# Delta rule: two chunks of a pair share their small operations, and a pair's inverses are fetched ahead of the doubling that reads them

## The chip, the cores and the metric

One NeuronCore of a Trainium2 chip runs one program. The metric is device time in microseconds (us), the median of a few executions; smaller is better. The engines are PE (TensorE, matrix products), DVE (VectorE), ACT (ScalarE), POOL (GpSimd) and SP (SyncE, which here only issues DMAs). Each runs its own instructions in a fixed order and waits on semaphores.

## The reference, cut to what matters

Two decoder layers over 2048 prompt tokens and 8 single sample tokens, everything in float32. The change concerns the gated delta rule of the first layer (4 heads of 128 channels; q, k, v, a decay g and a step beta per token). Per chunk of tokens:

```python
gc = jnp.cumsum(g, axis=-1)
decay = jnp.where(incl, jnp.exp(jnp.where(incl, diff, 0.0)), 0.0)
a_low = jnp.where(strict, jnp.einsum('bhnid,bhnjd->bhnij', kb, k) * decay, 0.0)
sol = lax.linalg.triangular_solve(a_low + jnp.eye(c), rhs, left_side=True, lower=True, unit_diagonal=True)
...
def step(s, xs):                       # over the chunks, one after the other
    v_new = u_n - w_n @ s
    o_n = qd_n @ s + qk_n @ v_new
    s = s * gl_n + kd_n.T @ v_new
```

q and k are l2-normalized before, and o is rms-normalized per token and head and multiplied by silu(z) after. The output then goes with a convolution branch through an output projection, followed by memory attention, a second layer and a last norm.

## The kernel before, in words

Large products run as three float32r products (high and low halves of both sides), so most of the time is PE time. The stages in order of time: products of the memory keys and values (to about 100 us), the input projection with its convolutions (to about 820 us), the delta rule (about 776 to 1208 us), the output projection `e2`, attention, the second layer.

Nothing is ordered by hand. A class `Flow` (line 56) keeps an estimated clock for every engine while the program is built. "Dense" code emits large products; side tasks are Python generators, and `pump` (line 342) steps a side task as soon as the estimate says that its inputs are there and its condition holds. So a changed size, condition or count moves instructions on all engines, and each engine then runs its list in that order whatever the real times are. `move` and `rows` (lines 191 and 201) put a copy on ACT or DVE by the estimated load, `ve` (line 210) on DVE or POOL. A DMA of a tile that only ACT wrote is issued by ACT, the others by SP.

The delta rule is `phase2` (line 1057), with 16 chunks of 128 tokens in 8 pairs. Beside it the dense work is `Fill` (line 990), 576 products that fold attention weights, the tiles `rhi` and `rlo` in the trace. The side tasks of the delta rule:

- `prep(n)` (line 1103), three at a time, one chunk each: loads k, q, v, forms the decay (`dec`), the matrix A = k k^T scaled by beta and the decay, and the products that the scan needs. The squared norms are in `ss`, and `br` holds four-column factors made by short DVE chains: a Newton inverse square root `rsqrt` (line 410, 11 DVE operations on [128, 4]) and five others. Chunks 0 to 3 may start when the pool `cq` is open; from chunk 4 on they need `dx`, which opens once the input projection has freed its last buffers.
- `inv16(t)` (line 1192): POOL inverts the 16x16 diagonal blocks of pair t.
- `levels(t)` (line 1215): sends these inverses into the tile `UT` by eight small DMAs, one per head and chunk, then doubles block size 16 to 32, 64, 128 on PE. One pair after the other.
- `scan()` (line 1295): the recurrence over the chunks, with the state in four tiles `S`.
- `onorms(i)` (line 1342), two tasks, one for even and one for odd chunks: the output norm, with 13 DVE operations on [128, 4], a multiplication by z, and a store to `d_b`.

`places` (line 1386) opens pools; `e2` can use its large tiles when all inverses are done, chunk 13 is scanned and the fill has ended.

Of the kernel before, what the change touches and what calls it, by code (L numbers as in the profile page):

```python
# [436 lines left out]
def spread(F, C, pool, ppool, r, n, tag, dg=None):  # L437
# [7 lines left out]
    ps = ppool.tile([128, 512], F32, tag="bg", name="ps_bc")  # L445
# [206 lines left out]
def phase1(F, C, I, D, st, P, R, mmp, bgp, loaders, mix, hp):  # L652
# [269 lines left out]
    def conv4(b, t):  # L922
# [11 lines left out]
        F.dma(D.qkv[b][:, t * 512:(t + 1) * 512], z)  # L934
# [122 lines left out]
def phase2(F, C, I, D, st, P, fill, hp, mmp, bgp, after):  # L1057
# [30 lines left out]
    slots, vfree = Res(SL), Res(3)  # L1088
# [1 line left out]
    done = {"A": set(), "T": set(), "L": set(), "S": {-1}, "N": set(), "P": set(), "U": set()}  # L1090
# [203 lines left out]

    def scan():
# [5 lines left out]
        for n in range(16):  # L1301
# [40 lines left out]
    def onorms(i):  # L1342
        for n in range(i, 16, 2):
            yield lambda: n in oq
            o, ss = oq.pop(n)
# [1297 lines left out]
```

## Time and profile before

| | us |
|---|---|
| median of 3 runs (2899.82 to 2907.46) | 2905.99 |
| the profiled execution | 2902.86 |
| its span, first to last instruction | 2901.1 |

Of the span PE is busy 2730.5 us, DVE 1968.4, ACT 1032.0 and POOL 657.0. Busy PE time is counted at the clock that PE was granted, so a slow stretch reads as busy. The profiled execution is 3.1 us under the median.

### The profile page before, as it was taken

To read this page: it belongs to the slowest core of one execution; us is meant where nothing else is said; L and a number is where in the kernel's file an instruction comes from. 1 tells how busy PE (TensorE), PEld (TensorE's weight loads), DVE (VectorE), ACT (ScalarE), POOL (GpSimd) and SP (SyncE) were. 2 spreads that over 40 slices of the span, in tenths; PEclk is the share of its full clock that TensorE was granted. 3 is DMA by queue.
4 is the path that set the end of the run, shared out by engine and by line. 5 is a ranking of instruction groups with operands and counts; after the bars stand their busy time and mean duration, and the time that the engine had idled before them with its cause. 6 is when DMAs were issued, how large, how long until landed. Compare 5 with 4: busy or idle time off the path is not lost.

```text
span 2901.1 us, 52440 instructions
## 1 busy us (share of the span) xinstructions
PE 2730.5 (94%) x20202; PEld 2498.5 (86%) x20202; DVE 1968.4 (68%) x4612; ACT 1032.0 (36%) x2448; POOL 657.0 (23%) x936
## 2 busy tenths in 40 slices
PE   7999999999998889799999999899999998999997
PEld 6878888888888778699898889899999997789987
DVE  6838999988667887776655556867755445765453
ACT  5632232233356455432321325443422122432321
POOL 3301112111054355122232320111011111221210
PEclk9999999999989899899999999999999999999998
DMA  7611122123455557565645434322545556422211
GB/s 240 213 48 41 46 75 65 46 77 113 129 148 160 154 165 230 172 228 183 211 149 169 144 117 140 116 70 74 173 134 165 181 165 206 136 78 68 70 59 52
DMA packets 269194, 377.85 MB, mean 130 GB/s; under 512 B 46096, under 2 KB 168208, under 8 KB 268944
## 3 DMA queue, kind: packets, MB, share of 16 engines
q1 hardware_dynamic: 211776, 264.77, 29.4%
q0 software_dynamic: 20864, 67.39, 7.5%
q10 hardware_dynamic: 36304, 42.34, 4.2%
q8 instruction: 159, 2.61, 0.4%
q14 instruction: 91, 0.75, 0.1%
HBM read 276.38 MB, written 96.40 MB: 128 GB/s over the span
## 4 chain that ended last, share of the span: by engine, by line
PE 34%; DMA 9%; DVE 6%; issue 2%; ACT 1%; POOL 1%; DVEq 0%; SPq 0%; POOLq 0%; ACTq 0%
PE ps_mm L168 32%; DMA a_big<-d_sp 2%; DVE a_big L225 1%; DMA a_big<-d_sq 1%; DMA a_big<-in_cache_v 1%; PE ps_pt L172 1%; DMA w_f<-d_x 1%; DVE rlo L225 1%; DVE w_d L219 1%; DMA rraw<-d_VW 1%; PE ps_row L168 1%; DVE rlo L219 1%; DVE ml L219 0%; DMA rraw<-d_G 0%; DMA a_big<-in_cache_k 0%
## 5 line engine op out<-in xcount | busy, mean ns | idle before, releaser
L219 POOL TENSOR_TENSOR rlo<-rraw,rhi 128x512 fp32r<-128x512 f32 x143 | 209.1, 1470 | 579.0 <-ACT rhi L186 495.5
L225 DVE SCALAR_TENSOR_TENSOR cacc<-glu,dww,cacc 128x1024 f32<-128x1024 f32 x240 | 325.6, 1369 | 5.9 <-ACT cacc L186 1.4
L219 POOL TENSOR_TENSOR w_sqb<-w_sqb,w_sqq 128x512 f32<-128x512 f32 (+1 forms) x101 | 137.1, 1357 | 660.9 <-ACT w_sqq L186 653.9
L168 PE MATMUL ps_mm<-xh,rhi 128*128 128x256 f32 (+1 forms) x1920 | 274.0, 285 | 5.3 <-DVE pool_sm L219 3.2
L168 PE MATMUL ps_mm<-xl,rhi 128*128 128x256 f32 (+1 forms) x1920 | 273.1, 284 | 0.0
L168 PE MATMUL ps_mm<-xh,rlo 128*128 128x256 f32 (+1 forms) x1920 | 272.7, 283 | 0.0
L168 PEld LDWEIGHTS ps_mm<-xh,rhi 128*128 128x128 f32 x1920 | 250.6, 192 | 8.6 <-issue 3.4
L168 PEld LDWEIGHTS ps_mm<-xl,rhi 128*128 128x128 f32 x1920 | 250.0, 192 | 2.6
L168 PEld LDWEIGHTS ps_mm<-xh,rlo 128*128 128x128 f32 x1920 | 248.2, 191 | 1.0
L168 PE MATMUL ps_mm<-hh,rhi 128*128 128x512 f32 (+2 forms) x1152 | 216.8, 329 | 20.2 <-ACT hh L186 15.8
L219 DVE TENSOR_TENSOR w_y<-ps_mm,w_y 128x256 f32<-128x256 f32 (+1 forms) x248 | 103.4, 420 | 165.6 <-PE ps_mm L168 161.2
L168 PE MATMUL ps_mm<-hh,rlo 128*128 128x512 f32 (+2 forms) x1152 | 214.6, 328 | 0.0
L168 PEld LDWEIGHTS ps_mm<-hh,rhi 128*128 128x128 f32 x1152 | 177.9, 191 | 42.0 <-ACT hh L186 16.2
L168 PE MATMUL ps_mm<-hl,rhi 128*128 128x512 f32 (+2 forms) x1152 | 211.7, 326 | 0.0
L225 DVE SCALAR_TENSOR_TENSOR a_big<-a_big 128x256 f32<-128x256 f32 x256 | 105.0, 448 | 144.5 <-DMA a_big<-d_sp 78.3
L186 ACT ACTIVATE rhi<-rraw 128x512 fp32r<-128x512 f32 x235 | 143.8, 628 | 164.0 <-DMA rraw<-d_G 41.5
L168 PEld LDWEIGHTS ps_mm<-hh,rlo 128*128 128x128 f32 x1152 | 175.9, 191 | 19.4 <-issue 2.2
L168 PEld LDWEIGHTS ps_mm<-hl,rhi 128*128 128x128 f32 x1152 | 175.4, 190 | 17.3
L168 PE MATMUL ps_mm<-mh,rhi 128*128 128x256 f32 (+1 forms) x1152 | 170.1, 288 | 11.8 <-ACT mh L186 11.7
L168 PE MATMUL ps_mm<-ml,rhi 128*128 128x256 f32 (+1 forms) x1152 | 170.5, 290 | 2.5 <-DVE ml L219 2.5
L168 PEld LDWEIGHTS ps_mm<-mh,rhi 128*128 128x128 f32 x1152 | 153.6, 195 | 14.5 <-ACT mh L186 12.8
L168 PE MATMUL ps_mm<-mh,rlo 128*128 128x256 f32 (+1 forms) x1152 | 165.6, 284 | 0.0
(425 smaller groups left out, 5344.5 us busy)
## 6 DMA issues: line engine op xcount, KB each, us to landing
w_f<-d_x SPq DMA_DIRECT2D x60, 512.0 KB
d_x<-w_y SPq DMA_DIRECT2D x44, 512.0 KB
w_y<-d_x SPq DMA_DIRECT2D x44, 512.0 KB
a_big<-in_cache_k POOLq DMA_DIRECT2D x64, 256.0 KB, 4.0
a_big<-in_cache_v POOLq DMA_DIRECT2D x64, 256.0 KB, 4.1
rraw<-in_w_in SPq DMA_DIRECT2D x56, 256.0 KB
d_qkv<-so ACTq DMA_DIRECT2D x48, 256.0 KB
rraw<-in_w_xk SPq DMA_DIRECT2D x32, 256.0 KB
```

The source lines that it names most:

```text
L168: self.nc.tensor.matmul(out, lhsT, rhs, start=start, stop=stop)
L172: self.nc.tensor.transpose(out, in_, ident)
L186: self.nc.scalar.activation(out=out, in_=in_, func=func, scale=scale, **kw)
L219: self._e(eng).tensor_tensor(out=out, in0=a, in1=b, op=op)
L225: self._e(eng).scalar_tensor_tensor(out=out, in0=a, scalar=s, in1=b, op0=op0, op1=op1, **kw)
```

## The change

1. The eight squared norms of a pair stand in one tile `ss`, interleaved by head and chunk, and all chains in `br` run once a pair on [128, 8], in the prep of the odd chunk. The even chunk waits for it (`done["K"]`, `done["B"]`, `done["R"]`). `onorms(t)` handles a pair too.
2. A new task `spread16(t)` does the eight DMAs into `UT` (now two buffers) ahead of `levels(t)`, which waits for an entry in `uts`.
3. The buffers of the late pool `dx` serve chunks 6 and 7 of each eight in place of 4 and 5, so chunks 4 and 5 may start before `dx` opens.
4. q, k, v, z and b lie in DRAM so that a chunk's four heads are one 2 KB run a partition (q, k, v, z) when read. The writers (`fin_z`, `conv4`) now write runs of 512 bytes in place of 2 KB, and `fin_z` issues more DMAs.
5. `spread` takes its PSUM pool from the work object at the time of use.

```diff
@@ fin_z, conv4 @@
-            F.dma(D.z[b][:, o:o + n], z[:, 0:n])
+            a = o
+            while a < min(o + n, SEQ):
...
+                    F.dma(D.z[c:c + k, :, b, :].rearrange("c p t -> p c t"), z[:, a - o:a - o + 128 * k].rearrange("p (c t) -> p c t", c=k))
...
-        F.dma(D.qkv[b][:, t * 512:(t + 1) * 512], z)
+        F.dma(D.qkv[b // 4, 4 * t:4 * t + 4, :, b % 4, :].rearrange("c p t -> p c t"), z.rearrange("p (c t) -> p c t", c=4))
@@ room, prep @@
-        q, b = (dx, 2) if n % 8 in (4, 5) else (cq, SL - 2)
+        q, b = (dx, 2) if n % 8 in (6, 7) else (cq, SL - 2)
...
-        yield lambda: nxt[0] == n and cq and (n < 4 or dx) and slots.n >= 2 - n % 2 and (n < SL or n // 2 - (SL+1)//2 in done["T"])
+        yield lambda: nxt[0] == n and cq and (n < 6 or dx) and slots.n >= 2 - n % 2 and (n < SL or n // 2 - (SL+1)//2 in done["T"])
...
-        F.dma(X.k, qkv[1][:, :, tok])
+        F.dma(X.k, D.qkv[1, n])
...
-        yield
+        done["K"].add(n)
+        yield lambda: n - c2 in done["K"]
...
-        br = X.br = cq.tile([128, 12], F32, tag="br", name="br", bufs=SL)
-        F.ts(br[:, 0:4], ss[:, 4:8], EPS, ALU.add)
-        F.recip(br[:, 4:8], br[:, 0:4])
-        F.tt(br[:, 4:8], br[:, 4:8], st.beta[:, :, n], ALU.mult)
-        F.stt(br[:, 8:12], br[:, 4:8], -1.0, gate["egc"][:, :, n], ALU.mult, ALU.mult)
+        if c2:
+            br = X.br = hu[n - 1].br = cq.tile([128, 32], F32, tag="br", name="br", bufs=SL // 2)
+            F.ts(br[:, 0:8], ss[:, 8:16], EPS, ALU.add)
+            F.recip(br[:, 8:16], br[:, 0:8])
...
+            done["B"].add(n // 2)
...
-        yield
+        yield lambda: n // 2 in done["B"]
...
-        rsqrt(F, cq, br[:, 4:8], br[:, 0:4], 4, "pr")
-        F.tt(br[:, 4:8], br[:, 4:8], st.beta[:, :, n], ALU.mult)
-        yield
+        if c2:
+            rsqrt(F, cq, br[:, 24:32], br[:, 0:8], 8, "pr")
...
+            done["R"].add(n // 2)
+        yield lambda: n // 2 in done["R"]
@@ levels @@
+    uts = {}
+
+    def spread16(t):
+
+        yield lambda: lp and t in done["T"] and (t < 2 or 2 * t - 4 in done["L"])
         ux = hu[2 * t].ux
-        UT = lp.tile([128, 8, 48], F32, tag="UT", name="UT", bufs=NL)
+        UT = lp.tile([128, 8, 48], F32, tag="UT", name="UT", bufs=2)
         F.memset(UT[:, :, 32:48], 0.0)
         for g in range(8):
             F.dma(UT[:, g, 0:32], ux[8 * g:8 * g + 8].rearrange("p r t k -> p r (t k)"))
+        uts[t] = UT, F.cur
+        F.now()
         done["U"].add(t)
+
+    def levels(t):
+        yield lambda: t in uts
+        U = A = hu[2 * t].A2.rearrange("p c h j -> p (c h) j")
+        UT, F.cur = uts.pop(t)
@@ onorms @@
-    def onorms(i):
-        for n in range(i, 16, 2):
-            yield lambda: n in oq
...
-            rsqrt(F, sq, f, os, 4, f"o{i}")
+    def onorms(t):
+        yield lambda: {2 * t, 2 * t + 1} <= set(oq)
...
+        rsqrt(F, sq, f, os, 8, "o")
@@ build @@
-        D.qkv = dr.tile([12, 128, SEQ], F32, name="d_qkv")
-        D.z = dr.tile([4, 128, NT], F32, name="d_z")
+        D.qkv = dr.tile([3, 16, 128, 4, 128], F32, name="d_qkv")
+        D.z = dr.tile([16, 128, 4, 128], F32, name="d_z")
+        D.zs = dr.tile([128, 4, 8], F32, name="d_zs")
...
-        D.b = [dr.tile([4, 128, gn(g)], F32, name=f"d_b{g}") for g in range(NG)]
+        D.b = [dr.tile([128, 4, gn(g)], F32, name=f"d_b{g}") for g in range(NG)]
```

What the planner makes of it, at three places. On DVE, the chain of `rsqrt` in one prep of the first chunks; `br` are the factors, `rt` and `ri` its scratch. Before:

```order
L415 TENSOR_SCALAR ri<-br 128x4
L234 TENSOR_SCALAR br<-ri 128x4
L219 TENSOR_TENSOR rt<-br 128x4
L225 SCALAR_TENSOR_TENSOR rt<-rt,br 128x4
L225 SCALAR_TENSOR_TENSOR br<-rt,br 128x4
L219 TENSOR_TENSOR rt<-br 128x4
L225 SCALAR_TENSOR_TENSOR rt<-rt,br 128x4
L225 SCALAR_TENSOR_TENSOR br<-rt,br 128x4
L219 TENSOR_TENSOR rt<-br 128x4
L225 SCALAR_TENSOR_TENSOR rt<-rt,br 128x4
L225 SCALAR_TENSOR_TENSOR br<-rt,br 128x4
L219 TENSOR_TENSOR br<-br,beta 128x4
```

and with the change:

```order
L415 TENSOR_SCALAR ri<-br 128x8
L234 TENSOR_SCALAR br<-ri 128x8
L219 TENSOR_TENSOR rt<-br 128x8
L225 SCALAR_TENSOR_TENSOR rt<-rt,br 128x8
L225 SCALAR_TENSOR_TENSOR br<-rt,br 128x8
L219 TENSOR_TENSOR rt<-br 128x8
L225 SCALAR_TENSOR_TENSOR rt<-rt,br 128x8
L225 SCALAR_TENSOR_TENSOR br<-rt,br 128x8
L219 TENSOR_TENSOR rt<-br 128x8
L225 SCALAR_TENSOR_TENSOR rt<-rt,br 128x8
L225 SCALAR_TENSOR_TENSOR br<-rt,br 128x8
L219 TENSOR_TENSOR br<-br,beta 128x8
```

The chain keeps its 12 operations, on eight columns in place of four, and stands once for two chunks. Over the program DVE has 4193 instructions in place of 4358: 232 fewer of these small ones, and 67 more of other kinds, mostly copies that the planner takes from ACT. PE has the same 18457.

On PE, where the second preps begin; `ident,gc` and `ident,k` are the first matmuls of a chunk, `hh` and `hl` the last group of the input projection, `rhi`/`rlo` the fill. Before, chunks 4, 5 and 6 begin together after the fill has started:

```order
L168 MATMUL ps_mm<-rhi,rlo 128x512 x2
L168 MATMUL ps_bg<-b_7977 32x32 x16
L168 MATMUL ps_bg<-ident,gc 128x128 x4
L172 MATMUL ps_bg<-ident,k 128x128 x4
L168 MATMUL ps_bg<-ident,gc 128x128 x4
L172 MATMUL ps_bg<-ident,k 128x128 x4
L168 MATMUL ps_bg<-ident,gc 128x128 x4
L172 MATMUL ps_bg<-ident,k 128x128 x4
```

With the change chunks 4 and 5 begin inside the last group of the input projection:

```order
L168 MATMUL ps_mm<-hl_236,rhi 128x260 x8
L168 MATMUL ps_mm<-hh_235,rlo 128x260 x8
L168 MATMUL ps_bg<-ident,gc 128x128 x4
L172 MATMUL ps_bg<-ident,k 128x128 x4
L168 MATMUL ps_mm<-hh_235,rhi 128x260 x4
L168 MATMUL ps_bg<-ident,gc 128x128 x4
L172 MATMUL ps_bg<-ident,k 128x128 x4
L172 MATMUL ps_bg<-ident,q 128x128 x4
```

The first matmul of chunk 4 has 54 fill products ahead of it before, and none with the change; 146 of the large products that stood ahead of it now stand behind.

On PE, the end of the delta stage; `S` is the state, `vn` the new values, `xh` and `xl` the first products of `e2`. Before, the last chunk's scan stands directly ahead of `e2`, and the last fill product 35 rows above `xh`:

```order
L168 MATMUL ps_bg<-S_7426,q_12977 128x128
L168 MATMUL ps_bg<-S_7427,q_12977 128x128
L168 MATMUL ps_bg<-S_7428,q_12977 128x128
L168 MATMUL ps_bg<-x,A 128x128 x4
L168 MATMUL ps_mean<-w_sqa,ones 128x256
L168 MATMUL ps_bg<-vn,kd 128x128 x4
L168 MATMUL ps_bg<-vn,qk 128x128 x4
L172 MATMUL ps_bg<-ident,o 128x128 x4
L168 MATMUL ps_ss<-ones,w_sqa 128x64 x2
L168 MATMUL ps_mm<-xh,rhi 128x264 x8
```

With the change the fill reaches to `e2`:

```order
L168 MATMUL ps_mm<-rhi,rlo 128x512 x2
L168 MATMUL ps_mm<-rhi 128x512 x2
L168 MATMUL ps_mm<-rlo,rhi 128x512 x2
L168 MATMUL ps_mm<-rhi,rlo 128x512 x2
L168 MATMUL ps_bc<-w_sqq,ones 128x256
L168 MATMUL ps_mm<-rhi 128x512 x2
L168 MATMUL ps_mm<-rlo,rhi 128x512 x2
L168 MATMUL ps_mm<-rhi,rlo 128x512 x2
L172 MATMUL ps_bg<-ident,o 128x128 x4
L168 MATMUL ps_mm<-xh,rhi 128x264 x8
L168 MATMUL ps_mm<-xl,rhi 128x264 x8
```

The last scan product (`vn,qk`) now has 36 fill products behind it, before none; the last product of the last pair's inverse has 168 behind it, before none.

## Rows read from the trace of the kernel before

**Rows 1.** The page, part 1 (busy us, share of the span, instructions) and the line of part 2 that gives the granted TensorE clock in tenths in 40 slices of 72.5 us.

```profile
PE 2730.5 (94%) x20202; PEld 2498.5 (86%) x20202; DVE 1968.4 (68%) x4612; ACT 1032.0 (36%) x2448; POOL 657.0 (23%) x936
...
PEclk9999999999989899899999999999999999999998
```

**Rows 2.** Busy time of each engine by stretch (from:to, length, then busy us and instructions of PE, PEld, DVE, ACT, POOL; then the granted clock, the DMA engines' mean busy share, GB/s).

```profile
820.00:1164.00 344.00, 299.52 (x3726) 268.96 (x3724) 264.14 (x811) 192.22 (x653) 169.37 (x324) 0.91 0.61 174
1164.00:1200.40 36.40, 23.35 (x175) 21.12 (x175) 29.62 (x74) 19.42 (x50) 5.55 (x6) 0.76 0.59 177
1200.40:1240.00 39.60, 34.06 (x247) 33.13 (x247) 28.32 (x72) 15.98 (x31) 2.84 (x3) 0.92 0.50 164
1240.00:1440.00 200.00, 194.58 (x1493) 184.45 (x1491) 137.72 (x311) 67.22 (x113) 55.36 (x64) 1.00 0.66 215
```

**Rows 3.** Who ended the idle time of PE between 820 and 1200.4 us: us in total, times, longest.

```profile
PE ps_bg L168 <- DVE S L225: 11.3, 5, 4.3
PE ps_bg L168 <- DVE lo L232: 9.7, 4, 4.3
PE ps_bg L168 <- DVE A L232: 8.9, 4, 3.3
PE ps_bg L168 <- ACT vn L186: 5.7, 3, 3.1
...
PE ps_bg L168 <- DVE x L225: 3.0, 2, 2.6
```

**Rows 4.** PE in order of time at the end of the delta stage: start, us, what, and in brackets the idle time before it.

```profile
1164.04 0.69 PE L168 MATMUL ps_bg<-b 32*32 32x32 f32 x32
1168.07 0.65 PE L168 MATMUL ps_bg<-A 64*64 64x64 f32 x8 [3.33 <-DVE A L232]
...
1187.63 1.26 PE L168 MATMUL ps_bg<-x,A 128*128 128x128 f32 x8 [2.61 <-DVE x L225]
...
1199.54 1.12 PE L168 MATMUL ps_ss<-ones,w_sqa 128*128 128x64 f32 x4 [4.96 <-POOL w_sqa L219]
1200.41 2.11 PE L168 MATMUL ps_mm<-xh,rhi 128*128 128x264 f32 x8
```

**Rows 5.** DVE groups by form between 820 and 1240 us: the small operations on four numbers a partition (count, busy us, mean ns, idle before).

```profile
L225 DVE SCALAR_TENSOR_TENSOR of<-rt,of 128x4 f32<-128x4 f32 x48 | 12.0, 249 | 1.7
...
L225 DVE SCALAR_TENSOR_TENSOR rt<-rt,os 128x4 f32<-128x4 f32 x48 | 10.2, 212 | 1.6
...
L225 DVE SCALAR_TENSOR_TENSOR br<-rt,br 128x4 f32<-128x4 f32 x36 | 8.7, 242 | 1.2
L225 DVE SCALAR_TENSOR_TENSOR rt<-rt,br 128x4 f32<-128x4 f32 x36 | 8.5, 237 | 1.2
L234 DVE TENSOR_SCALAR ss<-ss 128x4 f32<-128x4 f32 x16 | 8.4, 526 | 0.0
...
L219 DVE TENSOR_TENSOR br<-br,beta 128x4 f32<-128x4 f32 x24 | 8.2, 341 | 0.8
```

**Rows 6.** DVE in order of time within one such chain, then one row of POOL from the same microseconds.

```profile
972.06 0.16 DVE L225 SCALAR_TENSOR_TENSOR rt<-rt,br 128x4 f32<-128x4 f32 x1
972.26 0.16 DVE L225 SCALAR_TENSOR_TENSOR br<-rt,br 128x4 f32<-128x4 f32 x1
...
973.43 2.73 DVE L225 SCALAR_TENSOR_TENSOR br<-rt,br 128x4 f32<-128x4 f32 x1
976.19 0.17 DVE L219 TENSOR_TENSOR br<-br,beta 128x4 f32<-128x4 f32 x1
...
973.66 2.48 POOL L219 TENSOR_TENSOR rlo<-rraw,rhi 128x512 fp32r<-128x512 f32 x2
```

**Rows 7.** DVE, the whole trace, by form: the same operation on eight numbers a partition, from the sample group.

```profile
L225 DVE SCALAR_TENSOR_TENSOR a_r<-rt,a_r 128x8 f32<-128x8 f32 x9 | 1.5, 167 | 0.3
```

**Rows 8.** DVE groups by form between 820 and 1240 us: operations that a planner can put on DVE or ACT (POOL for the second).

```profile
L238 DVE CAST rhi<-rraw 128x512 fp32r<-128x512 f32 x38 | 18.3, 493 | 1.8 <-DMA rraw<-in_w_xqT 1.8
...
L219 DVE TENSOR_TENSOR rlo<-rraw,rhi 128x512 fp32r<-128x512 f32 x24 | 16.8, 715 | 2.7 <-ACT rhi L186 2.7
...
L232 DVE TENSOR_SCALAR gv<-ps_mm,g_x 128x256 f32<-128x256 f32 x23 | 10.6, 480 | 9.3 <-DMA d_G<-gv 7.0 <-ACT gv L186 2.0 <-DMA d_VW<-gv 0.3
...
L238 DVE COPY ad<-A 32x128 f32<-32x128 f32 x22 | 5.5, 252 | 0.3
...
L238 DVE COPY b<-ps_bg 32x256 f32<-32x256 f32 x10 | 4.0, 411 | 2.3 <-PE ps_bg L168 2.0 <-ACT b L186 0.2
```

**Rows 9.** The tile UT, whole trace: its DMA issues on SP (ns min/median/max of one issue, first and last).

```profile
L313 SPq DMA_DIRECT2D UT<-x x64: 604/605/867, 817.9 to 1139.6; - x64
```

**Rows 10.** DMA queues (packets, MB, share of 16 engines): SP's between 820 and 1200.4 us, then ACT's between 200 and 700 us; then a wait of ACT between 200 and 820 us.

```profile
q1 hardware_dynamic: 89594, 56.82, 52.4%
...
q10 hardware_dynamic: 8928, 14.75, 8.1%
...
ACT so L186 <- DMA d_qkv<-so: 4.2, 2, 2.2
```

**Rows 11.** ACT between 820 and 1240 us: the group that rounds weights, with what ended its idle time.

```profile
L186 ACT ACTIVATE rhi<-rraw 128x512 fp32r<-128x512 f32 x58 | 35.8, 630 | 31.6 <-DMA rraw<-in_w_out_e 9.2 <-DMA rraw<-in_w_xqT 7.0 <-DMA rraw<-d_G 5.3
```

**Rows 12.** PE: the first matmuls of chunk 6 and of chunk 7, partners of one pair, in order of time.

```profile
844.25 1.33 PE L168 MATMUL ps_bg<-ident,gc 128*128 128x128 f32 x8 [2.51 <-DVE A L232]
...
896.10 1.06 PE L168 MATMUL ps_bg<-ident,gc 128*128 128x128 f32 x8
```

More of the change, by code (lines that the diff above doesn't have):

```diff
@@ L444, in spread @@
     yield
-    ps = ppool.tile([128, 512], F32, tag="bg", name="ps_bc")
+    ps = getattr(ppool, "bgp", ppool).tile([128, 512], F32, tag="bg", name="ps_bc")
     F.mm(ps[:, 0:n], C.ones, dg[:, 0:n])
@@ L772, in fin_z @@
             F.act(z[:, 0:n], ps[:, 0:n], AF.Silu)
-            F.dma(D.z[b][:, o:o + n], z[:, 0:n])
+            a = o
+            while a < min(o + n, SEQ):
+                c, r = divmod(a, 128)
+                e = min(o + n, SEQ)
+                if r == 0 and e - a >= 128:
+                    k = (e - a) // 128
+                    F.dma(D.z[c:c + k, :, b, :].rearrange("c p t -> p c t"), z[:, a - o:a - o + 128 * k].rearrange("p (c t) -> p c t", c=k))
+                    a += 128 * k
+                else:
+                    k = min(128 - r, e - a)
+                    F.dma(D.z[c, :, b, r:r + k], z[:, a - o:a - o + k])
+                    a += k
+            if o + n > SEQ:
+                F.dma(D.zs[:, b, :], z[:, SEQ - o:NT - o])
         fin = {"z": fin_z}
@@ L1087, in phase2 @@
     SL = 8
[L1088 removed]
+    slots, vfree, afree = Res(SL), Res(3), Res(3)
     nxt = [0]
[L1090 removed]
+    done = {"A": set(), "T": set(), "L": set(), "S": {-1}, "N": set(), "P": set(), "U": set(), "B": set(), "R": set(), "K": set()}
     inext = [0]
@@ L1108, in prep @@
         X.ia = cq.tile([64, 16, 16], F32, tag="a16", name="a16", bufs=(SL + 1) // 2) if n % 2 == 0 else hu[n - 1].ia
+        ss = X.ss = cq.tile([128, 16], F32, tag="ss", name="ss", bufs=8) if n % 2 == 0 else hu[n - 1].ss
         X.A2 = room("A", n) if n % 2 == 0 else hu[n - 1].A2
         X.A = X.A2[:, n % 2]
-        tok = slice(128 * n, 128 * n + 128)
         X.k = room("k", n)
@@ L1123, in prep @@
         F.tt(dec, C.negm.unsqueeze(1).to_broadcast([128, 4, 128]), pd, ALU.subtract)
-        ss = X.ss = cq.tile([128, 8], F32, tag="ss", name="ss", bufs=16)
+        c2 = n % 2
         pk = ps4()
@@ L1151, in prep @@
         for h in range(4):
-            F.stt(X.A[:, h, :], pa[:, h, :], br[:, 4 + h:5 + h], dec[:, h, :], ALU.mult, ALU.mult)
-        yield vfree.ok
+            F.stt(X.A[:, h, :], pa[:, h, :], br[:, 8 + 2 * h + c2:9 + 2 * h + c2], dec[:, h, :], ALU.mult, ALU.mult)
+        yield lambda: vfree.ok() and afree.ok()
         vfree.take()
+        afree.take()
         v = small("v", 2 * NP, 3)
-        F.dma(v, qkv[2][:, :, tok])
+        F.dma(v, D.qkv[2, n])
         F.now()
@@ L1174, in prep @@
             F.dma(X.ia[i:i + 8], a16[:, h, :])
+        afree.give()
         done["A"].add(n)
@@ L1187, in prep @@
         X.bv = room("bv", n)
-        F.rows(X.bv, pv, br[:, 4:8])
+        F.rows(X.bv, pv, hk(br[:, 24:32])[:, :, c2])
         vfree.give()
@@ L1340, in scan @@
             F.dma(D.o_delta_p[h], S[h])
[L1342 to L1347 removed]
+    def onorms(t):
+        yield lambda: {2 * t, 2 * t + 1} <= set(oq)
+        os = sq.tile([128, 8], F32, tag="os", name="os", bufs=1)
+        o, z = [], []
+        for c in range(2):
+            oc, ss = oq.pop(2 * t + c)
+            o.append(oc)
+            z.append(sq.tile([128, 4, 128], F32, tag=f"z{c}", name="z", bufs=1))
+            F.dma(z[c], D.z[2 * t + c])
             F.now()
[L1349 removed]
+        for c in range(2):
             for h in range(4):
                 j = sq.tile([128, 128], F32, tag="junkq", name="junkq", bufs=1)
[L1352 removed]
+                F.act(j, o[c][:, h, :], AF.Square, accum=os[:, 2 * h + c:2 * h + c + 1])
             yield
[L1355 to L1360 removed]
+        F.ts(ss[:, 0:8], ss[:, 0:8], EPS, ALU.add, EPS * 128, ALU.mult)
+        F.stt(os, os, 1.0 / 128, ss[:, 0:8], ALU.mult, ALU.add)
+        f = sq.tile([128, 8], F32, tag="of", name="of", bufs=1)
+        rsqrt(F, sq, f, os, 8, "o")
+        yield
+        for c in range(2):
+            n = 2 * t + c
+            F.rows(o[c], o[c], f.rearrange("p (h c) -> p h c", c=2)[:, :, c])
             yield
@@ L1378, in phase2 @@
         F.spawn(every(levels, i, NL, 8), 2)
+    F.spawn(every(spread16, 0, 1, 8), 2)
     for i in range(NI):
         F.spawn(every(inv16, i, NI, 8), 2)
-    for i in range(2):
-        F.spawn(onorms(i), 1)
+    F.spawn(every(onorms, 0, 1, 8), 1)
     for i in range(NP):
@@ L1486, in tok_spread @@
 def tok_spread(F, C, W, r, n):
-    return spread(F, C, W.p, W.bgp, r, n, "w", dg=W.t("sqq", [128, ceil128(n)]))
+    return spread(F, C, W.p, W, r, n, "w", dg=W.t("sqq", [128, ceil128(n)]))
 def mm3(F, R, W, name, j, x, n):
```

41 lines of the change are left out of this document (16 added, 25 removed).

## The prediction, made before the changed kernel had run

> **What bounds the kernel now.** I read the page first: PE is busy 94% of the span, and its granted clock falls to eight tenths only in slices 12, 14 and 17 of 40, which lie between 798 and 1233 us, and in the last slice [rows 1]. That stretch is the delta stage. The table of stretches gives its losses. Busy time multiplied by the granted clock is about what the same work takes at full clock; what is left of a stretch's length is loss. 820 to 1164 us: 344.0 - 299.5 x 0.91 = 71.4 us lost. 1164 to 1200.4 us: 36.4 - 23.35 x 0.76 = 18.7. 1200.4 to 1240 us: 39.6 - 34.06 x 0.92 = 8.3. The 200 us after that lose 5.4 [rows 2]. So 98 us in the delta stage and its exit could be won, and PE's instructions are the same before and after: the change can only win idle time and slow clock.
>
> Whom does PE wait for? Mostly DVE: for S 11.3 us, lo 9.7, A 8.9, x 3.0, and for ACT's vn 5.7 [rows 3]. DVE is busy 264 of the 344 us, 77% [rows 2]. DMAs hardly appear among PE's waits. After 1164 us the fill is used up and PE has only the last pair's inverse and the last two scans, each step waiting for DVE, until the first product of e2 at 1200.41 [rows 4]. Its clock stood at 1.2 in place of 2.4 GHz for about half of that stretch, the mean granted clock being 0.76 [rows 2].
>
> **Part 1, the shared chains.** Per chunk 16 small DVE operations in prep and 13 in the output norm go: 29 x 16 = 464 on [128, 4] become 232 on [128, 8]. Eight columns cost no more than four: 167 ns in the sample group [rows 7] against 160 in an undisturbed chain, one every 0.20 us [rows 6]. In their groups they average more: six of them take 56.0 us for 208, 269 ns each [rows 5]. The excess is not their own work. An operation of 0.16 us took 2.73 and ended at 976.16; POOL's two 128x512 subtractions from 973.66 on ended at 976.14 [rows 6]. So 232 operations are worth 232 x 0.20 = 46 us if only their own time goes, and 232 x (0.269 + 0.036 of gap) = 71 us if the waits go with them. I take 46, since the subtraction on POOL stays and whichever DVE operation comes next would wait for it.
>
> The Trainium skill, page "SBUF — State Buffer", section "SBUF: two separate sides", has a rule on this: VectorE and GpSimd arbitrate for a shared pair of ports as an exclusive lock, held for a whole instruction, and the loser blocks fully. The row of 2.73 us looks like that. Taken strictly it speaks against this change: the lock time is set by POOL's work, not by the number of DVE operations. By it the sum keeps 46, without it 71.
>
> Against that, the planner puts 67 other operations on DVE: by the two programs 20 more ad, 10 b, 10 rhi, 8 gv, 6 rlo, at 0.252, 0.411, 0.493, 0.480, 0.715 us [rows 8], 22 us, and 13 mixed ones at up to 0.7 that partly cancel; I take 26 in all. Net, DVE is relieved of 46 - 26 = 20 us, between 20 and 45. ACT loses the copies that DVE gains; nothing on PE waits for ACT longer than 5.7 us in total, so I cost that at nothing. Of the 20 us I put on the path the share for which DVE is busy, 0.77: **-15 us**. Lower bound 0 (all of it turns into DVE idle time), upper 45 / 0.77 = 58.
>
> The new waits: the even chunk's A waits for the odd chunk's norms, and behind it in the same task stand its copies, its DMA to POOL's inverse and its qk. The order shows partners starting three PE rows apart, so this costs about one chunk's norms, covered by the third prep and by the levels of the pair before. I take nothing; its bad case is a rival below.
>
> **Part 2, the inverses fetched ahead.** Eight issues of 0.605 us on SP are 4.8 us [rows 9], plus the landing, between the end of the last pair and lo. They leave the chain; PE's wait for lo was 9.7 us in four times [rows 3]. The first pair's stays. Three quarters go: **-7 us**, bounds 0 and -9.7. What is late next is the scan's S, 11.3 us, which I leave.
>
> **Part 3, chunks 4 and 5 earlier, and the tail.** They start in the last group of the projection, before the fill. With the shorter chain all later delta work moves ahead of the fill: the last scan has 36 fill products behind it, the last inverse 168, before none. The tail of 36.4 us was loss because PE had nothing else; now the two last scans have fill between them. Its 18.7 us go: **-18.7 us**, bounds -9 (the fill runs out early, since DVE lags the planner's estimate) and -18.7.
>
> With the tail goes a cover. The first weights of e2 were loaded and rounded in it, and ACT already waited 9.2 us for them [rows 11]. The fill's last products now stand directly ahead of e2. Price between 0 and 9.2; I take **+4 us**.
>
> The norms ahead of e2 come earlier too, so of the 8.3 us lost after 1200.4 about half goes: **-4 us**, bounds 0 and -8.
>
> **Part 4, layouts.** SP's queue takes 0.524 x 380.4 x 16 / 89594 = 36 ns a packet in the delta stage, ACT's 0.081 x 500 x 16 / 8928 = 73 ns in the projection, where its packets are larger [rows 10]. Reads: five loads a chunk of 512 packets, 40960, become 10240: 40960 x 36 - 10240 x 73 ns over 16 engines, 45 us less load on engines that are 61% busy. PE did not wait for them, so 0. Writes: 48 stores of 128 packets become 512 each: 24576 x 36 - 6144 x 73 ns over 16 engines, 27 us more, in 500 us in which the DMA engines are about a fifth busy; ACT waits 4.2 us for these stores [rows 10]. If that doubled it would still lie beside a PE that has no gap there: 0, bound +4. The PSUM pool of the spread costs nothing: the same instruction.
>
> **The sum.** -15 - 7 - 18.7 + 4 - 4 = -40.7. Against the profiled execution's 2902.86 that is 2862.2; the median of the runs is 3.1 higher, so **2865 us**.
>
> **The rivals.** (a) **Only the tail goes.** The stage is paced by DVE standing behind POOL's subtractions, not by the number of small operations; a shorter chain meets the same subtractions. Then the 71.4 us between 820 and 1164 stay. -18.7 + 9.2 - 4 = -13.5: 2892. This is what the lock would do here. For it: the 2.73 us; against: PE's waits name scan and level steps, which queue behind the chains on DVE. The Trainium skill's page "SBUF — State Buffer" states that lock. (b) **The clock comes back.** Once PE's idle gaps are short, the clock stays at 2.4 GHz, and some 45 of the 71.4 us go: -45 - 18.7 - 8 = -72: 2834. For it: the granted clock is 1.00 from 1240 to 1440 us, where PE is busy 97% [rows 2]; against: waits on S and A remain. (c) **Slower: a held pair.** Chunk 6 started at 844.25 and its partner at 896.10, 52 us apart [rows 12]; before, that held nobody. If a partner lags so now, the even chunk, its inverse, and both scans wait, in an order that PE can't leave. One such lag on the path gives 2862 + 52 = 2914, with the 3.1 2917; from a lag of about 50 us on (40.7 and the 8.7 below) the result is slower. Against: the order starts partners together. (d) **It does little:** DVE's relief vanishes in the copies, and a new wait at the entry of e2 eats the tail: about 2905.
>
> **Chances.** My forecast, 2850 to 2880: 0.50. (a), 2880 to 2897: 0.22. (b), 2825 to 2850: 0.16. (c) 0.06. (d) 0.06. About 0.3%, 8.7 us, is what a measurement of this kernel can tell from no change, so faster is below 2897.3: 0.88; same 0.06; slower 0.06. A range from 2830 to 2897 takes in the forecast, (a) and most of (b) and leaves out (c), (d) and the best end of (b), with something for terms outside the delta stage, where the order shifts by a few rows.
>
> **What would show it.** Right: the DVE rows `rt<-rt,br` and `of<-rt,of` as 128x8, 24 each, near 0.17 to 0.27 us; PE's wait for lo below 4 us; no stretch of PE without `rhi` products ahead of the first `xh` product, and that product some 37 us earlier, near 1163 us; the stretch from 820 on with a granted clock above 0.91. Wrong: PE idle for lo, A or S as long as before, a clock under 0.9 between 820 and 1000 us where the delta work is now denser, or a wait of over 9 us for the weights `in_w_out_e` at the entry of e2; or a gain that the stretches after 1440 us give back.

## The result: 40 us slower

The change takes 2943.9 us (median of 4 runs, 2942.2 to 2955.2), the kernel before 2903.8 beside it (2899.8 to 2907.5): a ratio of 1.0144, 95% interval 1.0120 to 1.0167. The forecast was 2865, the range 2830 to 2897. The profiled execution of the change took 2945.1, its span 2943.4.

Page of the change, parts 1 and 2, as in [rows 1]:

```profile
PE 2732.1 (93%) x20202; PEld 2502.6 (85%) x20202; DVE 1950.4 (66%) x4447; ACT 1008.7 (34%) x2394; POOL 646.7 (22%) x929
...
PEclk9999999999998998799999999999999999999999
```

PE's work is the same, and DVE is relieved by 18.0 us; that part came as forecast. The stretches of the change, columns as in [rows 2]; the third is the one between the last fill product and the first of `e2`:

```profile
820.00:1164.00 344.00, 291.17 (x3729) 265.49 (x3727) 241.14 (x671) 169.49 (x579) 152.87 (x314) 0.90 0.52 154
1164.00:1203.30 39.30, 30.13 (x168) 26.40 (x168) 24.13 (x63) 20.83 (x61) 15.54 (x12) 0.83 0.72 224
1203.30:1223.30 20.00, 1.28 (x5) 0.73 (x5) 8.66 (x25) 8.62 (x22) 0.00 (x0) 0.63 0.57 168
1223.30:1265.00 41.70, 32.37 (x223) 31.46 (x223) 29.47 (x50) 13.39 (x27) 3.44 (x2) 0.85 0.64 204
```

Loss again as length less busy time multiplied by clock. 820 to 1164 us: 81.9, where before lost 71.4, although DVE was busy 23 us less. 1164 to 1203.3: 14.3, so the old tail's 18.7 are not gone either. Then 19.2 us of nearly nothing, and 14.2 in the 41.7 us after that (before: 8.3 in 39.6). PE's waits from 820 to 1223.4 us, as in [rows 3]:

```profile
PE ps_bg L172 <- ACT o L186: 18.7, 1, 18.7
PE ps_bg L168 <- DVE S L225: 8.9, 6, 2.0
PE ps_bc L168 <- DVE w_sqq L232: 7.8, 1, 7.8
PE ps_mm L168 <- ACT gv L186: 7.5, 2, 6.4
PE ps_bg L168 <- DVE A L232: 6.3, 2, 4.5
PE ps_bg L172 <- DMA v<-d_qkv: 5.2, 3, 4.3
PE ps_bg L172 <- DVE o L219: 4.5, 2, 4.2
...
PE ps_bg L168 <- ACT vn L186: 1.8, 2, 1.4
...
PE ps_bg L168 <- DVE lo L232: 0.8, 1, 0.8
```

The wait for `lo` is gone (9.7 to 0.8), and the waits for `S`, `A`, `vn` and `x` are smaller than in [rows 3]. In their place stand waits that were small or absent before: for the norms' `o`, for `w_sqq` of the norms ahead of `e2`, for the fill's `gv`, for a load of `v`. The hole at the end, on PE (as in [rows 4]), DVE, ACT and SP's queue, start and us:

```profile
1202.68 0.64 PE L168 MATMUL ps_mm<-rhi,rlo 128*128 128x512 f32 x2
1222.03 1.35 PE L172 MATMUL ps_bg<-ident,o 128*128 128x128 f32 x4 [18.72 <-ACT o L186]
```

```profile
1217.38 0.43 DVE L238 CAST rhi<-rraw 128x512 fp32r<-128x512 f32 x1 [9.80 <-DMA rraw<-in_w_out_e]
...
1218.89 0.17 DVE L234 TENSOR_SCALAR ss<-ss 128x8 f32<-128x8 f32 x1
...
1221.37 0.17 DVE L225 SCALAR_TENSOR_TENSOR of<-rt,of 128x8 f32<-128x8 f32 x1
```

```profile
1221.57 2.45 ACT L186 ACTIVATE o<-o,of 128x128 f32<-128x128 f32 x8 [1.26 <-DVE of L225]
```

```profile
1205.48 0.37 SPq L313 DMA_DIRECT2D d_VW<-gv  x1
1209.60 1.48 SPq L313 DMA_DIRECT2D w_y<-in_xT  x3
1211.13 1.45 SPq L313 DMA_DIRECT2D rraw<-in_w_out_e  x3
```

Read from the bottom: the loads of `w_y` start 4 us after the store of the fill's last `gv`, on whose memory their tiles lie. The weights `in_w_out_e` stand behind them in SP's queue, DVE's `rhi` waits 9.80 us for these weights, the paired norm of chunks 14 and 15 stands behind that `rhi`, ACT's `o` behind the norm, and PE's transposes of `o` stand ahead of the first `xh` product. By position in the program, the 5000th matmul into `ps_mm` starts 28.8 us later than before, the 6000th 29.6, the 7000th, in the first attention layer, 44.7, the last 42.5. So about 29 us arise up to the first products of `e2` and some 15 between 1404 and 1582 us.

### The profile page after: what moved, and what is told of

It is laid out like the page before. It is cut to its first block, busy times and chain, and to the rows that moved or that the text cites. A ratio compares the mean times of both kernels' runs of the same rounds, so it can differ in the third digit from the quotient of the medians.

```text
span 2943.4 us, 52205 instructions
## 1 busy us (share of the span) xinstructions
PE 2732.1 (93%) x20202; PEld 2502.6 (85%) x20202; DVE 1950.4 (66%) x4447; ACT 1008.7 (34%) x2394; POOL 646.7 (22%) x929
## 5 line engine op out<-in xcount | busy, mean ns | idle before, releaser
L219 POOL TENSOR_TENSOR rlo<-rraw,rhi 128x512 fp32r<-128x512 f32 x137 | 201.7, 1482 | 568.8 <-ACT rhi L186 498.4
L168 PEld LDWEIGHTS ps_mm<-hh,rhi 128*128 128x128 f32 x1152 | 178.0, 191 | 42.8 <-ACT hh L186 16.4
L186 ACT ACTIVATE rhi<-rraw 128x512 fp32r<-128x512 f32 x225 | 137.7, 627 | 186.9 <-DMA rraw<-d_VW 47.1
L168 PEld LDWEIGHTS ps_mm<-hh,rlo 128*128 128x128 f32 x1152 | 175.3, 190 | 19.2 <-issue 1.9
L168 PEld LDWEIGHTS ps_mm<-mh,rhi 128*128 128x128 f32 x1152 | 153.3, 195 | 11.2 <-ACT mh L186 9.2
```

The costliest lines, as they stand in the source:

```text
L168: self.nc.tensor.matmul(out, lhsT, rhs, start=start, stop=stop)
L186: self.nc.scalar.activation(out=out, in_=in_, func=func, scale=scale, **kw)
L219: self._e(eng).tensor_tensor(out=out, in0=a, in1=b, op=op)
```

## The experiments

Each kernel ran beside the kernel before; "first `xh`" and "5000th", "7000th" (against before) are from its profile, loss is that from 820 us to the first `xh` product. These columns are from one execution each, which can lie some us from the median (in g4 2929.7 us against 2938.3).

| | ratio to before, 95% | median us | last fill | first `xh` | loss | 5000th | 7000th |
|---|---|---|---|---|---|---|---|
| before | 1 | 2904 | 1164.1 | 1200.4 | 93 | 0 | 0 |
| the change | 1.0144 (1.0120 to 1.0167) | 2943.9 | 1203.3 | 1223.3 | 119 | +28.8 | +44.7 |
| e1 layouts only | 1.0028 (1.0012 to 1.0043) | 2914.0 | 1174.1 | 1202.8 | 94 | +4.0 | +13.5 |
| e2 layouts, places | 1.0030 (1.0011 to 1.0049) | 2910.5 | 1188.4 | 1195.2 | 87 | +1.1 | +16.4 |
| e3 change, no places | 1.0066 (1.0044 to 1.0087) | 2924.8 | 1199.4 | 1218.2 | 113 | +14.6 | +19.6 |
| e4 change, norms apart | 1.0060 (1.0042 to 1.0079) | 2925.0 | 1199.7 | 1203.9 | 94 | +11.2 | +27.1 |
| f1 change, ops back | 1.0293 (1.0264 to 1.0323) | 2988.0 | 1241.5 | 1262.2 | 162 | +70.9 | +79.6 |
| f2 last pair apart | 1.0116 (1.0087 to 1.0145) | 2934.6 | 1201.7 | 1209.2 | 103 | +24.8 | +39.0 |
| f3 `gv` kept | 1.0103 (1.0076 to 1.0131) | 2934.0 | 1205.2 | 1220.7 | 114 | +22.3 | +28.7 |
| g1 entry mended | 1.0067 (1.0050 to 1.0083) | 2920.2 | 1206.3 | 1213.5 | 102 | +11.6 | +14.6 |
| g2 UT on POOL's queue | 1.0137 (1.0120 to 1.0154) | 2940.1 | 1200.0 | 1219.8 | 115 | +25.9 | +37.7 |
| g4 change reordered | 1.0133 (1.0114 to 1.0153) | 2938.3 | 1187.5 | 1199.1 | 90 | +17.5 | +29.6 |
| f4 before reordered | 1.0057 (1.0040 to 1.0073) | 2918.2 | 1176.4 | 1202.4 | 99 | +7.2 | +11.2 |
| g3 before reordered | 1.0034 (1.0020 to 1.0048) | 2909.9 | 1167.0 | 1203.1 | 96 | +1.3 | +1.1 |
| h4 places, mended | 1.0028 (1.0012 to 1.0044) | 2912.5 | 1190.0 | 1194.3 | 82 | -1.9 | +10.8 |
| h8 norms apart, mended | 1.0061 (1.0040 to 1.0082) | 2918.5 | 1196.2 | 1199.9 | 88 | -2.1 | +18.4 |
| h7 before, `w_y` queue | 0.9983 (0.9967 to 0.9999) | 2899.9 | 1168.0 | 1203.2 | 93 | +1.5 | +3.1 |
| h1 before, fewer ops | 0.9965 (0.9951 to 0.9979) | 2892.4 | 1156.5 | 1188.3 | 81 | -14.2 | -11.5 |
| i1 before, joined | 0.9959 (0.9947 to 0.9972) | 2890.4 | 1153.2 | 1189.5 | 84 | -12.4 | -10.7 |
| i2 before, more ops | 1.0149 (1.0136 to 1.0162) | 2945.4 | 1204.7 | 1244.1 | 141 | +43.4 | +45.4 |

**The parts, one at a time (e1 to e4).** e1 keeps the layouts of the change and nothing else; e2 keeps the places too. e3 and e4 undo one part of the change:

```diff
@@ e3 @@
-        q, b = (dx, 2) if n % 8 in (6, 7) else (cq, SL - 2)
+        q, b = (dx, 2) if n % 8 in (4, 5) else (cq, SL - 2)
...
-        yield lambda: nxt[0] == n and cq and (n < 6 or dx) and slots.n >= 2 - n % 2 and (n < SL or n // 2 - (SL+1)//2 in done["T"])
+        yield lambda: nxt[0] == n and cq and (n < 4 or dx) and slots.n >= 2 - n % 2 and (n < SL or n // 2 - (SL+1)//2 in done["T"])
@@ e4: onorms(i) of before, on the change's layout @@
-    F.spawn(every(onorms, 0, 1, 8), 1)
+    for i in range(2):
+        F.spawn(onorms(i), 1)
```

> Theory of the entry: the loss is made where the fill's last product meets e2's first, because the turn-round of the pool and the first weights had the last two scans as their cover. With the layouts alone the two last scans still stand behind the fill, so there is no hole: within 8 us of before, 2896 to 2912, first xh product within 5 us of 1200. Rival, the layouts: loads of k, q, v and z on ACT's queue or the shorter runs of the stores hold PE; then most of the 40 us is here, 2935 to 2945. Rival, the order: any edit that moves the order costs tens of us; then 2915 to 2940 at scattered places.

> Layouts and the earlier start of chunks 4 and 5, no shared chains, no fetching ahead. By the order 120 fill products stand behind the last scan, so the delta rule is done well ahead of the fill. Theory of the entry: PE idle 12 to 20 us between the last fill product and the first xh product although no norm is late; 2905 to 2930, slower than e1 by 10 to 20. Rival, the shared chains: the loss comes from a pair's first chunk waiting for its second; then nothing is lost here, 2870 to 2895.

> The change with chunks 4 and 5 held back as before (rest as in the change). Six fill products stand behind the last scan. Theory of the entry: the hole stays, since the fill still ends last: 2925 to 2950, PE idle 15 us or more ahead of the first xh product. Rival, the earlier start is the cause: 2895 to 2910. Rival, shared chains: as the change, 2935 to 2950, but with the loss between 820 and 1200.

> The change with one output norm a chunk, as before. Theory of the entry: the pool and the weights set the first xh product, so the hole shrinks by at most 3 us and the time by 0 to 8: 2935 to 2945. Rival, the paired norm: the last chunk's norm behind its partner made the hole; then it falls to under 8 us and the time to 2915 to 2930.

The kernel with the layouts alone is about 8 us slower, little of it at the entry (first `xh` at 1202.8). With the places alone the fill ends last and PE waits only 6.8 us, not 12 to 20: ending the fill next to `e2` is not by itself the hole. With the norms apart PE waits 3.8 us for the last norm's `o`, and the median falls by 19. My theory of pool and weights alone fell here; the rival, the paired norm, was right on the hole. e3 keeps a gap of 18.8 us between the last fill product and the first `xh` (PE waits 7.7 us in it for `w_sqa` and 8.3 for `o`) with six fill products behind the last scan, so the gap does not need the early start. Still its median, too, is 19 us below the change's. No run separates what either part costs from the order that it brings.

**What a small operation is worth (f1, h1, i2).** All three leave every other row in its place, because the planner does not learn of the edit. `more(pool, x, k)` adds k operations without use on a scratch tile.

```diff
@@ f1, on the change (i2, on before: 8 and 6 a chunk, [128, 4]) @@
             rsqrt(F, cq, br[:, 24:32], br[:, 0:8], 8, "pr")
+            more(cq, br[:, 0:8], 16)
...
         rsqrt(F, sq, f, os, 8, "o")
+        more(sq, os, 13)
@@ h1, on before, in rsqrt @@
-    for _ in range(3):
+    for i in range(3):
+        if tag in ("pr", "o0", "o1") and i:
+            for _ in range(3):
+                F._op("dve", 4 / 0.96 + 68, [y], [y, t, x])
+            continue
```

> The change with the small operations that it saves put back as work without use: 16 a pair in prep and 13 a pair in the norms, 232 in all on [128, 8] of a scratch tile, at the place of the inverse square roots and unknown to the planner, so that every other row stands as in the change. It prices the shared chains alone. The prediction's term: 232 x 0.20 = 46 us of DVE, 0.77 of it on the path: 25 to 40 us slower than the change, 2965 to 2985. Rival, DVE's free time takes them: PE waits for single steps in a fixed order and not for DVE's total: 0 to 10 us slower, 2940 to 2955.

> The kernel before with two of the three Newton steps of the inverse square roots of prep and of the output norm left out (so q, k and o are scaled less exactly): 192 small DVE operations less, and every other row in the order of before, since the planner still counts them. Theory that the order lost the gain: each operation is worth its 0.19 us here as it was in the change, 36 us; 2866 to 2878. Rival, DVE's relief is worth nothing once PE's other waits are next: 0 to 10 us, 2892 to 2902. In between, at half the price, 2880 to 2890.

> The kernel before with 224 more small operations without use (8 a chunk in prep, 6 in the output norm, on [128, 4] of a scratch tile, unknown to the planner, every other row as before). Theory of the kink, an order made for a certain DVE time: less than that is left idle, more is waited for one for one: 0.15 to 0.2 us each, 34 to 45 us slower, 2938 to 2950. Rival, the two orders differ, and before has slack on DVE that the change lacks: 0.05 us each, 8 to 15 us slower, 2912 to 2920.

Added, an operation costs its full time: 1.0293 - 1.0144 of 2903 is 43 us for 232, 0.19 us each; in before 0.0149 of 2904 is 43 us for 224, 0.19. Taken away, 192 gave 0.0035 of 2905, 10.2 us (6 to 14), 0.05 each. The two rows from 820 to 1164 us, h1 first, then i2, against the first of [rows 2]:

```profile
820.00:1164.00 344.00, 296.49 (x3804) 267.53 (x3803) 237.66 (x670) 196.32 (x660) 169.36 (x322) 0.93 0.62 179
```

```profile
820.00:1164.00 344.00, 277.96 (x3340) 251.38 (x3338) 272.70 (x909) 174.25 (x601) 154.35 (x312) 0.85 0.53 151
```

In h1 DVE is busy 26 us less and PE loses 68.3 us in place of 71.4: most of the freed time became idle time of DVE, which fits rows of PE that stand where the plan put them. In i2 the same engine is late, and PE's waits for DVE grow (820 to 1240 us, top rows):

```profile
PE ps_bg L168 <- DVE S L225: 19.1, 5, 5.6
PE ps_bg L168 <- DVE x L225: 12.8, 4, 7.6
PE ps_bg L168 <- DVE lo L232: 10.1, 5, 4.6
```

In before `S` cost 11.3 and `x` 3.0 [rows 3]. The granted clock falls with it, 0.91 to 0.85. From 820 us to the first `xh` product, columns as in [rows 2], before, then h1, then i2:

```profile
820.00:1200.40 380.40, 322.87 (x3900) 290.07 (x3899) 293.76 (x884) 211.64 (x702) 174.92 (x330) 0.89 0.61 175
820.00:1188.30 368.30, 312.67 (x3893) 282.25 (x3892) 257.48 (x719) 212.10 (x702) 172.24 (x324) 0.92 0.62 179
820.00:1244.10 424.10, 337.20 (x3907) 302.96 (x3905) 330.92 (x1079) 212.69 (x703) 173.01 (x331) 0.84 0.54 157
```

PE's idle time, length less busy time, is 57.5, 55.6 and 86.9 us. So of i2's 44 us here 29 are waiting and 14 are longer busy time for much the same products, at a lower granted clock; of h1's 12 only 2 are less waiting, and 10 are shorter busy time at a higher clock.

**The entry (f2, f3, g1, h7).** f2 does chunks 14 and 15 one norm at a time (`apart` has the same steps, chunk by chunk on four columns); f3 puts `gv` into a pool that stays open; g1 has both, and `w_y` over POOL's queue, which is all that h7 does to before.

```diff
@@ f2 @@
     def onorms(t):
+        if t == 7:
+            yield from apart(t)
+            return
@@ f3 @@
-                    g = wp.tile([128, 512], F32, tag="gv", name="gv", bufs=2)
+                    g = self.gp.tile([128, 512], F32, tag="gv", name="gv", bufs=2)
@@ g1 = f2 + f3 + this; h7 = before + this; in _dma @@
+        if out.tensor.name.startswith("w_y") and in_.tensor.name.endswith("xT"):
+            eng = "gpsimd"
```

> The change with the output norms of chunks 14 and 15 alone done one at a time; up to the last fill product the rows are the same. Theory of the pair at the entry: chunk 14's norm no longer stands behind the weights on DVE and its transposes leave the way of the first xh product; the hole of 18.7 us falls to 5 to 10, 2930 to 2936. Rival, pool and weights: the first xh product still waits for the weights loaded behind w_y, so it starts within 2 us of the change's 20 us after the last fill product; 2940 to 2946.

> The change with the fill's result tile gv in a pool that stays open, so that the tiles of e2 don't lie on it and their loads don't wait for its last store. Same rows up to the entry. Theory of the pool: the loads w_y and behind them the weights go out about 4 us earlier, at 1205.5 in place of 1209.6, and the hole shrinks by 4 to 8 us: 2934 to 2942. Rival, the paired norm: DVE's row of the last pair's norm decides, and it stands behind the same weights: no change, 2940 to 2947. The order after the entry shifts, which alone may give 10 us either way after 1400 us.

> The change with the last pair's norms apart, gv in a pool that stays open, and the loads w_y<-in_xT issued by POOL's queue in place of SP's, where the weights of e2 stood behind them. Same rows as in the change up to the last fill product. Theory of the entry, two causes one behind the other (the paired norm, then weights behind w_y): hole under 6 us, and no wait over 3 us for weights in the next 40 us; first xh product 1205 to 1209, product 5000 at 1249 to 1254 against 1267 in the change; 2918 to 2930. Rival: the weights' own landing is the limit whatever their place in the queue; product 5000 at 1259 or later, 2930 to 2940.

> The kernel before with w_y loaded over POOL's queue, all else in its order. Here the two last scans cover the first weights, so the entry theory expects little: 0 to 5 us faster, 2896 to 2904. If instead this alone brings 10 us or more, the queue costs time everywhere and not at the entry.

f2 alone moves the wait. PE's rows there, the hole first, then a stop inside the first product:

```profile
1207.69 1.11 PE L172 MATMUL ps_bg<-ident,o 128*128 128x128 f32 x4 [5.99 <-DVE o L219]
1209.25 1.25 PE L168 MATMUL ps_mm<-xh,rhi 128*128 128x264 f32 x4 [0.44 <-ACT xh L186]
1217.01 1.25 PE L168 MATMUL ps_mm<-xh,rhi 128*128 128x264 f32 x4 [6.52 <-ACT xh L186]
```

The first `xh` product comes 14 us sooner, but 10 of them are given back by the 5000th. f3 alone sends the `w_y` loads at 1205.23 in place of 1209.60, PE's wait for `o` falls from 18.7 to 14.4, and the median from 2943.9 to 2934.0. With all three edits, in g1, the gain stays:

```profile
1212.75 1.12 PE L172 MATMUL ps_bg<-ident,o 128*128 128x128 f32 x4 [6.46 <-DVE o L219]
```

In g1 the 5000th comes 17 us sooner than in the change, with 6.46 us of hole and 1.6 us at most in one wait after it (the expectation named 1205 to 1209 for the first `xh`; it came at 1213.5, 3 us of which are the fill, which ended later in that run). The rest of g1's 24 us lies after 1400 us. In before, where two scans cover the weights, the queue is worth about 5 us (0 to 10) by the medians; its profiled execution does not show them at the entry (first `xh` 2.8 us later).

**The fetch ahead (g2).**

```diff
+        if out.tensor.name.startswith("UT"):
+            eng = "gpsimd"
```

> The change with the eight loads into UT issued by POOL and not by SP; every other row stands as in the change. Theory of SP's queue: fetching ahead put these loads, 4.6 us of issues, ahead of the fill's store of gv (issued at 1099.09, 6.6 us after its tile was written), and PE lost 6.4 us at 1098.9 to it, and more in smaller pieces; 6 to 12 us faster than the change, 2931 to 2938, PE's wait for gv under 3 us. Rival, nothing: the wait moves to the next step, 2940 to 2947; or POOL's issues delay rlo and it gets slower.

A miss: 2940, and PE still lost 4.9 us for `gv` at the same place. SP's rows say why: the store of `gv` goes out only behind a load for the norms of `e2`, whose turn comes at 1099.93 also without the UT loads:

```profile
1092.33 0.37 SPq L315 DMA_DIRECT2D d_G<-gv  x1
1099.93 0.37 SPq L315 DMA_DIRECT2D w_c<-d_c  x1
1100.35 0.50 SPq L315 DMA_DIRECT2D w_f<-d_sg  x1
1100.90 0.50 SPq L315 DMA_DIRECT2D d_G<-gv  x1
```

So that wait belongs to the queue's order, not to the fetch ahead.

**Order by itself (f4, g3, g4).** The same work, save a few copies that change between ACT and DVE (DVE has 4607 and 4605 instructions where before has 4612), with the planner's look-ahead moved: in before to 3900 ns (f4, shown) and 3600 (g3), in the change to 3400 (g4).

```diff
-        F.LIM = (1500.0, 3800.0, 1000000000.0)
+        F.LIM = (1500.0, 3900.0, 1000000000.0)
```

> The kernel before with one constant of the planner moved, by which a side task may run 3900 ns ahead of PE and not 3800 during the fill: the same instructions in another order (about a sixth of the rows move). It prices order by itself. Theory of the order: the before is a picked order, and a neutral shift costs 5 to 20 us: 2910 to 2925, part of it between 1400 and 1550 us. Rival, order is worth little: within 6 us of before, 2899 to 2911.

> The kernel before with the planner's look-ahead at 3600 ns in place of 3800: same instructions, another order. Theory of the order: before is one of the best of its family, so this one too is 5 to 20 us slower, 2910 to 2925. Rival: the shift to 3900 was unlucky; within 5 us of before, 2898 to 2908.

> The change with the look-ahead at 3400 ns: same instructions, another order. Theory of the order: the change is an unlucky member of a family that lies 10 to 20 us on either side; 2920 to 2940. Rival: the change is slow by construction (pairs, the end of the fill next to e2) whatever the order; 2938 to 2955.

The two other orders cost before 10 and 17 us, and the third gives the change some 3 (the intervals of the ratios overlap). In g4 the hole is gone (first `xh` at 1199.1) and comes back inside `e2`: the 5000th product is 17.5 us late.

**Can the parts win once the entry is mended (h4, h8)?** e2 and e4, each with f3's edit and the queue of h7.

> The places alone (with the layouts, without pairs and without fetching ahead) and a mended entry: gv in a pool that stays open, w_y loaded over POOL's queue. Theory of the entry: of the 6.8 us hole, the 14 us lost in the next 40 us and the 10 to 15 us after 1400 most go, as they did in the change: 2885 to 2897, faster than before. Rival: the order after the entry is a draw of its own, 2898 to 2912.

> The change with one output norm a chunk and the mended entry (against the change with mended entry and paired norms, save the last pair, 2920; and against norms apart with the entry as it is, 2925). Theory of the entry: 15 to 25 us less than 2925: 2900 to 2910. Rival, the norms' pairing saves 104 operations, worth 20 us by the price of the runs: 2925 to 2940, slower than with pairs.

A miss for the entry theory in both (2885 to 2897 and 2900 to 2910 were expected). At the 5000th product both are 2 us ahead of before; they lose 13 and 20 us from there to the 7000th and end 8 and 18 us slower. The change has such a second loss too. PE's waits in the change from 1430 to 1500 us, then in before from 1395 to 1465, the same part of the first attention layer:

```profile
PE ps_pt L172 <- DVE xl L219: 6.1, 2, 5.2
PE ps_ss L168 <- POOL w_sqa L219: 5.5, 1, 5.5
```

```profile
PE ps_ss L168 <- POOL w_sqa L219: 2.9, 1, 2.9
PE ps_pt L172 <- DVE xl L219: 0.5, 1, 0.5
```

ACT has a row ahead of the wait for `w_sqa`, where a weight came late and the squares that `w_sqa` sums stood behind it:

```profile
1434.17 0.63 ACT L186 ACTIVATE rhi<-rraw 128x512 fp32r<-128x512 f32 x1 [9.80 <-DMA rraw<-d_VW]
```

From the 5000th to the 7000th product the change, e2, e4, f2, g2, g4, h4 and h8 lose 11.8 to 20.5 us, and e1, where the entry is nearly as in before, 9.5; the kernels with before's order, e3, f4, g1 and g3 lose at most 5 (f1 and f3 lie between, 8.7 and 6.4). Neither the places nor the pairs decide it: e1 has neither and has the loss, g1 has both (save the last pair's norm) and lacks it. That it comes with an order is what is left, but is not shown: every kernel that has the loss also has the new layouts, and no run tells these from the order.

**What helped, joined (i1).** h7's edit, and one Newton step of three left out in prep and the output norm (h1 left out two; in both, q, k and o are scaled a little less exactly).

> The kernel before with w_y over POOL's queue (5 us faster alone) and one of three Newton steps left out in prep and the output norm (the last one, so the scales of q, k and o are a little less exact): 96 operations less in an unchanged order. At 0.05 us an operation 5 us, with the queue 10: 2890 to 2898. If operations are worth 0.19 us once others are gone: 2880 to 2888. If the queue's 5 us were chance: 2896 to 2902.

2890.4, a ratio of 0.9959 (0.9947 to 0.9972): faster than both kernels, and it keeps before's order.

## Why the prediction was wrong

In losses of the profiled executions, the terms for the tail, the chains and the fetch, -40.7 together, came as +6.1: 96.2 us from 820 us to the last fill product, where before lost 90.1 up to the first `xh`. The two terms of the entry, 0 together, came as +25.1: 19.2 of hole, and 14.2 in place of 8.3 behind it. The first attention layer, not in the sum, came as +15.

1. **The tail, -18.7.** The step that failed first: a wait that moves under the fill was counted as won. The scans did move ahead of the fill, and PE's waits for `S`, `lo`, `A`, `vn` and `x` did fall, from 38.6 us together to 17.8. But others took their place (`w_sqq` 7.8, `gv` 7.5, `v` 5.2, DVE's `o` 4.5), and the granted clock stayed low (0.90 where before had 0.91, 0.83 up to the last fill product). With the entry mended the loss from 820 us to the first `xh` product is 82 (h4), 88 (h8) and 102 (g1), against 93: 11 us were won at best, by the places alone, 5 with the paired chains of prep, and nothing with paired norms too. Those kernels differ in order too, so how much each part does is not settled.
2. **The cover of the tail, +4, bounded at 9.2.** The mechanism was named, the size was wrong: 18.7 us of hole, and 14.2 lost after it where before lost 8.3. The prediction's own sign came, over 9 us of wait for `in_w_out_e`: 9.80. The bound came from ACT's wait for weights that had a cover [rows 11]; without it the chain is store, pool, `w_y`, weights, rounding, norm, transposes, one behind the other. I counted the shared chain in the norms only as fewer operations, not as a wait of chunk 14 for chunk 15 at the place where nothing hides it. Mending this gave back 24 of the 40 us (g1), 17 of them at the entry; g1's other 12 us up to the 5000th product stay open.
3. **The shared chains, -15.** DVE was relieved as forecast (20 us from 820 us to the first `xh` product, 18.0 over the run), at 0.17 us an operation. The share on the path was wrong for taking away: 10.2 of 192 x 0.20 = 38 us is 0.27, not 0.77. By that, 20 us are worth 5. 0.77, DVE's busy share, says nothing of it, nor does the upper bound of 58, which divides by it where the term multiplies. (The gap of 0.036 us in the prediction's 71 is 6.5 us over 208 in the rows, 0.031; the sum does not use it.)
4. **The fetch ahead, -7.** PE's wait for `lo` went from 9.7 to 0.8 as forecast; no run separates what it brought in time.
5. **The norms earlier, -4.** They were not: 14.2 us lost after the entry.
6. **The layouts, 0, bound +4.** About 8 us in e1, but later than the delta stage and within what a new order alone costs (f4, g3). That DMAs cause it is not shown.
7. **Outside the stage: "a few rows".** Two new orders of the kernel before cost 10 and 17 us by themselves, and kernels with the new layouts lost up to 20 in the first attention layer, the change 15; the cause there stays open between layouts and order. A cost of the order itself was the missing case in the chances; rival (d) had the place (entry of `e2`), not the size; rival (c) had the sign, but the chunk that waited for its partner was that of the last norm, not one in prep: for `A` PE waited 6.3 us, less than before.

Rival (a) took DVE to be paced by POOL's subtractions, by the exclusive lock of the shared ports (the Trainium skill, "SBUF — State Buffer", section "SBUF: two separate sides"). It speaks against a gain from fewer operations, and the gain was small. But a stage paced so would have taken added operations cheaply as well, and they cost their full time. The kink between taking away and adding fits the fixed order, and part of it is clock; no run separates the two.

## What to carry to other kernels

In an order fixed before the run, price an engine's time twice: more of it is paid in full, less of it mostly turns to idle time until the rows that wait for it are moved. Before moving a tail under other work, list what the tail covered (here a pool's turn-round, a queue, weights and the last norm) and follow that chain with its cover gone. And run a neutral reordering of the kernel first: where that costs 10 to 17 us, as here, the sum of an edit's parts is no forecast to better than that.

## What was not expected of the hardware

232 operations of 0.17 us (median, f1) added to an engine that was busy 70% of the stretch (241.14 of 344 us) lengthened the run by 43 us, 0.19 us each. Part of such a price is clock: in i2 the mean granted clock was 0.84 from 820 us to the first `xh` product, in h1 0.92, before 0.89, and PE's busy time for about the same instructions was 337.2, 312.7 and 322.9 us.
